# Half of an encoder block's output projection by Strassen's seven products, the sums of weights made by accumulating DMAs

## The chip, the cores and the metric

The kernel runs on one core of a Trainium2 chip. The metric is the device time of one execution in microseconds; the time of the kernel before is the median of three runs, 913.6 us (913.25 to 913.76).

## The reference

One layer of a hybrid encoder block on 256 tokens of width 2048, in float32:

```
xn     = rms_norm(x, norm_pre_w)
z      = xn @ w_in                       # 2048 x 13312: u, g_lru, q, k, v, g_attn, m_lru, m_attn
y_a    = rg_lru(conv(u)) * silu(g_lru)   # both directions, added
y_b    = windowed_gqa(q, k, v) * silu(g_attn)
merged = sigmoid(m_lru) * (y_a @ w_proj_a) + sigmoid(m_attn) * (y_b @ w_proj_b)
x      = x + rms_norm(merged @ w_out, norm_post_w)
```

The change concerns `merged @ w_out` (256 x 2048 by 2048 x 2048) and what surrounds it. The last norm needs the sum of squares of a token's whole row of 2048, so nothing of a token's output can be written before its last column is there.

## The kernel before

Every float32 operand of a matmul is cut in two float32r parts, high and low (`parts_of`, `split`), and each product is three matmuls (`mm3`, L165: high by high, high by low, low by high). ScalarE (ACT) casts the high part, VectorE (DVE) subtracts for the low part.

The program is a list of steps, one for each 1 MB load of weights in `load_plan`, in the order in which TensorE (PE) uses them. A step has two half-steps; PE works on one half (1024 columns of the loaded tile) in each. The loop at the end of `body` writes the program out half-step by half-step: `fetch` issues the load of three steps ahead on SyncE's (SP's) queue, into a ring of three buffers `raw`; then come the callbacks that are due at this half-step (`at`, `soon`); then `split` cuts the half that is four half-steps ahead into `wh` and `wl`, rings of five buffers; then the matmuls. Each engine takes its own instructions strictly in that order.

`add_rows` adds a column chunk of 512 of a projection with tokens as rows: four steps of kind "quad", each of which holds four blocks of 128 rows of the weights; per step 4 blocks x 2 halves of the tokens x 3 = 24 matmuls of 128x512. It takes two PSUM banks for a chunk, from the ring of four single banks `bg` (`bank`, `spare=True`) or as one of two double tiles `mm` (`banks`).

The end of the program, in order: chunks of `w_proj_b` (`add_pb`) alternate with the last gates (`add_ma`). After each `w_proj_b` chunk, `turn` transposes the merged tile on PE in two pieces into a `bg` bank `mt` and cuts it into the tiles `ms` (eight in all: 256 rows of the contraction by 256 tokens, high and low part), which are the operand of the output projection. Then four chunks `o0` to `o3` of `w_out` follow (16 steps, tile name `o`), each evacuated by `o_evac`: ACT squares with a running sum (`junk`, L723), DVE multiplies by the norm's weight (`yw`, L726). In the last chunk the matmuls of the second half of the tokens come after the first half's are complete (`held`), so that the first half's ending runs beside them. The ending of a token half is a square root, a reciprocal and four scaled additions of the input rows `xr` (L738), each with its output DMA. `load_tail` loads `npt` and `xr` from the second half-step of the projection on. Tiles of 4 KB a partition are taken from the pool `u` of 31 units; a unit that is reused waits for its last reader.

Of the kernel before, what the change touches and what calls it, by code (L numbers as in the profile page):

```python
# [14 lines left out]
F32 = mybir.dt.float32  # L15
F32R = mybir.dt.float32r
# [4 lines left out]
P = 128  # L21
# [21 lines left out]
       ("w_proj_a", 1536), ("w_in", MA0), ("w_in", MA0 + 512)]  # L43


PV_NORM = 0
PV_CW = 16
PV_CB = PV_CW + 64
# [7 lines left out]
def load_plan():  # L56

    plan = []

    def quad(m, c):  # L60
        plan.extend(("quad", m, c, i) for i in range(4))

    def pair(m, c, n):
        plan.extend(("blk", m, c + (n + i) * P, 0) for i in range(2))

    quad("w_in", U0)
    for i in range(8):
# [19 lines left out]
    for c in range(4):  # L87
        quad("w_out", c * 512)
    return plan


def body(ctx, tc, x, xT, wall, wlru, pvec, npost, ident_d, mask_d, rope_d, out):
# [8 lines left out]
    def unit(name, dt=F32, shape=(P, 4, S)):  # L101
        return units.tile(list(shape), dt, tag="u", name=name)
# [17 lines left out]
    def parts_of(h, l, src, cast=nc.scalar.copy):  # L120
        cast(h, src)
        nc.vector.tensor_tensor(l, src, h.bitcast(F32), ALU.subtract)
# [8 lines left out]
    def at(hs, fn):  # L131
        assert hs >= now[0], (hs, now[0])
        due.setdefault(hs, []).append(fn)
# [8 lines left out]


    raws, parts = {}, {}

    def fetch(i):
# [3 lines left out]
        nc.sync.dma_start(raws[i], wall[i])  # L150

    def split(q, c=0, w=1024, cast=nc.scalar.copy, only=None):
        i, h = q // 2, q % 2
        if i >= len(plan):
            return
        if c == 0 and only != "l":
            parts[q] = [ring.tile([P, 1024], F32R, tag=f"w{s}", name=f"w{s}{i}_{h}", bufs=5) for s in "hl"]
        wh, wl = parts[q]
        hs, ls, raw = wh[:, c:c + w], wl[:, c:c + w], raws[i][:, h * 1024 + c:h * 1024 + c + w]
        if only != "l":  # L160
            cast(hs, raw)  # L161
        if only != "h":
            nc.vector.tensor_tensor(ls, raw, hs.bitcast(F32), ALU.subtract)  # L163
# [41 lines left out]
    def add_rows(name, act, done, spare=False, last=False):  # L205


        got, held = [], []

        def products(t, g, h, wh, wl):  # L210
            ts = slice(t * P, (t + 1) * P)
            for j in range(2):
                k = 4 * g + 2 * h + j
                sl = slice(j * 512, (j + 1) * 512)
                a = act[k // 2][:, k % 2, :, ts]
                mm3(got[t], a[:, 0], a[:, 1], wh[:, sl], wl[:, sl], k == 0, k == KT - 1)

        def half(g, h, wh, wl):
            if g == 0 and h == 0:
                if spare:  # L220
                    got.extend(bank(f"{name}{t}", (P, 512)) for t in range(2))
                else:
                    ps = banks(name, (P, 2, 512))
                    got.extend(ps[:, t] for t in range(2))
            products(0, g, h, wh, wl)
            if last and g >= 2:
                held.append((1, g, h, wh, wl))
            else:
                products(1, g, h, wh, wl)
            if g == 3 and h == 1:  # L230
                if last:
                    done(0, got[0])
                    for a in held:
                        products(*a)
                    done(1, got[1])
                else:
                    soon(lambda: [done(t, got[t]) for t in range(2)])

        for g in range(4):
            steps.append(("quad", lambda h, wh, wl, g=g: half(g, h, wh, wl)))  # L240


    pv = const.tile([P, PV_N], F32, name="pv")
# [267 lines left out]
            nc.vector.tensor_tensor(dst, dst, sg, ALU.mult)  # L511
        return done

    tm, sm, ms = [], [], []


    def gate_evac(units_list, c):
# [146 lines left out]
    def add_pb(c):  # L664
        def done(t, ps):
            g = sm[c][:, t]
            nc.vector.tensor_tensor(g, ps, g, ALU.mult)
            nc.vector.tensor_tensor(g, tm[c][:, t], g, ALU.add)
            if t == 1:
                for i in range(2):  # L670
                    soon(lambda i=i: turn(i), i + 1)

        def turn(i):

            ps = bank(f"mt{c}{i}")
            for j in range(2):
                sl = slice((2 * i + j) * P, (2 * i + j + 1) * P)
                for t in range(2):
                    nc.tensor.transpose(ps[:, j, t * P:(t + 1) * P], sm[c][:, t, sl], ident)
            m = pair_unit(f"ms{2 * c + i}")  # L680
            ms.append(m)
            parts_of(m[:, :, 0], m[:, :, 1], ps)

        add_rows(f"pb{c}_", yb, done)

# [19 lines left out]

    def load_tail():
        for h in range(2):
            sl = slice(h * 1024, (h + 1) * 1024)
            npt.append(unit(f"np{h}", F32, (P, 1024)))
            nc.sync.dma_start(npt[h], npost[:, sl])  # L710
            for t in range(2):
                xr[t].append(unit(f"xr{t}{h}", F32, (P, 1024)))
                yw[t].append(unit(f"yw{t}{h}", F32, (P, 1024)))
                nc.sync.dma_start(xr[t][h], x[t * P:(t + 1) * P, sl])

    at(2 * len(steps) + 2, load_tail)

    def o_evac(c):
        def done(t, ps):
            cs = slice((c % 2) * 512, (c % 2 + 1) * 512)  # L720
            junk = small.tile([P, 512], F32, tag="p", name=f"junk{c}{t}", bufs=2)
            sums, bb = so[t], bias[t]
            nc.scalar.activation(junk, ps, AF.Square, accum_out=sums[:, c:c + 1])  # L723
            if c == 3:
                nc.scalar.activation(bb, sums[:, 3:4], AF.Sqrt, scale=1.0 / D, bias=bb)
            nc.vector.tensor_tensor(yw[t][c // 2][:, cs], ps, npt[c // 2][:, cs], ALU.mult)  # L726
            if c == 2:
                nc.vector.tensor_tensor(sums[:, 0:1], sums[:, 0:1], sums[:, 1:2], ALU.add)
                nc.vector.tensor_tensor(sums[:, 0:1], sums[:, 0:1], sums[:, 2:3], ALU.add)
                nc.vector.tensor_scalar(bb, sums[:, 0:1], 1.0 / D, EPS, ALU.mult, ALU.add)  # L730
                if t == 1:
                    nc.scalar.activation(warm, eps, AF.Sqrt)
            if c == 3:
                nc.vector.reciprocal(bb, bb)
                for q in range(4):
                    cs = slice((q % 2) * 512, (q % 2 + 1) * 512)
                    y = yw[t][q // 2][:, cs]
                    nc.vector.scalar_tensor_tensor(y, y, bb, xr[t][q // 2][:, cs], ALU.mult, ALU.add)  # L738
                    eng = nc.sync if q % 2 == 0 else nc.scalar
                    eng.dma_start(out[t * P:(t + 1) * P, q * 512:(q + 1) * 512], y)  # L740
        return done

    for c in range(4):
        add_rows(f"o{c}_", ms, o_evac(c), True, c == 3)


    assert [s[0] for s in steps] == [p[0] for p in plan]
    for i, (_, half) in enumerate(steps):
        for h in range(2):
            now[0] = hs = 2 * i + h  # L750
            if h == 0:
                fetch(i + 3)
# [16 lines left out]

def pack_weights(w):  # L770
    loads = []
    for kind, m, c, i in load_plan():
        if kind == "quad":
# [58 lines left out]
```

## Time and profile before

| | |
|---|---|
| median of three runs | 913.6 us |
| the profiled execution, its own time | 914.62 us |
| its span, first to last instruction | 912.8 us |
| PE busy | 903.2 us (99%), 4790 matmuls |
| DVE busy | 650.6 us (71%) |
| ACT busy | 534.7 us (59%) |
| GpSimd (POOL) busy | 1.4 us |
| DMA | 172.20 MB, mean 189 GB/s |
| granted TensorE clock | 0.998 |

Engines work at the same time, so the busy times are not to be added. Matmuls are pipelined: one is shown as 0.39 us long, but the next starts before it ends, so what a matmul costs PE is the distance between two starts. The span leaves out 1.8 us of the profiled execution's time, before the first and after the last instruction.

### The profile page before, as it was taken

To read this page: it belongs to the slowest core of one execution; us is meant where nothing else is said; L and a number is where in the kernel's file an instruction comes from. 1 tells how busy PE (TensorE), PEld (TensorE's weight loads), DVE (VectorE), ACT (ScalarE), POOL (GpSimd) and SP (SyncE) were. 2 spreads that over 40 slices of the span, in tenths; PEclk is the share of its full clock that TensorE was granted. 3 is DMA by queue.
4 is the path that set the end of the run, shared out by engine and by line. 5 is a ranking of instruction groups with operands and counts; after the bars stand their busy time and mean duration, and the time that the engine had idled before them with its cause. 6 is when DMAs were issued, how large, how long until landed. Compare 5 with 4: busy or idle time off the path is not lost.

```text
span 912.8 us, 12138 instructions
## 1 busy us (share of the span) xinstructions
PE 903.2 (99%) x4790; PEld 775.5 (85%) x4790; DVE 650.6 (71%) x900; ACT 534.7 (59%) x744; POOL 1.4 (0%) x23
## 2 busy tenths in 40 slices
PE   8999999999999999999999999999999999999996
PEld 8898888888888888888888888888888888888885
DVE  6976968697879888898687868666555555555554
ACT  7678586859497967855644545644464434344451
POOL 0000000000000000000000000000000000000000
PEclk9999999999999999999999999999999999999999
DMA  9764465445464454456544445454555555558532
GB/s 334 257 236 170 162 223 185 165 181 208 155 238 174 162 207 150 154 215 230 186 163 159 145 179 174 150 179 145 183 191 201 183 204 182 191 192 315 185 139 92
DMA packets 27609, 172.20 MB, mean 189 GB/s; under 512 B 3072, under 2 KB 3840, under 8 KB 8480
## 3 DMA queue, kind: packets, MB, share of 16 engines
q1 hardware_dynamic: 26688, 170.14, 52.5%
q10 hardware_dynamic: 864, 1.29, 0.4%
q8 instruction: 37, 0.61, 0.3%
q14 instruction: 20, 0.16, 0.1%
HBM read 169.32 MB, written 2.10 MB: 188 GB/s over the span
## 4 chain that ended last, share of the span: by engine, by line
PE 98%; DMA 1%; DVE 0%; ACT 0%; DVEq 0%; ACTq 0%; issue 0%
PE ga L190 7%; PE q L190 7%; PE gl L190 6%; PE u L190 5%; PE o L166 4%; PE o L167 4%; PE o L168 4%; PE ga L189 3%; PE q L189 3%; PE gl L189 3%; PE u L189 2%; PE u_ps L358 2%; PE k L190 2%; PE gate L166 1%; PE gate L167 1%; PE gate L168 1%
## 5 line engine op out<-in xcount | busy, mean ns | idle before, releaser
L163 DVE TENSOR_TENSOR wl<-raw,wh 128x1024 fp32r<-128x1024 f32 (+1 forms) x306 | 370.1, 1214 | 206.6 <-ACT wh L161 206.1
L161 ACT CAST wh<-raw 128x1024 fp32r<-128x1024 f32 (+1 forms) x305 | 315.5, 1045 | 202.5 <-PE o L168 33.1
L190 PE MATMUL ga<-xs,wh 128*128 128x512 f32 x256 | 90.1, 396 | 0.0
L190 PE MATMUL q<-xs,wh 128*128 128x512 f32 x256 | 89.7, 396 | 0.0
L190 PE MATMUL gl<-xs,wh 128*128 128x512 f32 x224 | 78.9, 397 | 0.0
L190 PE MATMUL u<-xs,wh 128*128 128x512 f32 x192 | 67.6, 396 | 0.0
L189 PE MATMUL ga<-xs,wl 128*128 128x256 f32 x240 | 67.2, 280 | 0.0
L189 PE MATMUL q<-xs,wl 128*128 128x256 f32 x240 | 67.0, 279 | 0.0
L189 PE MATMUL gl<-xs,wl 128*128 128x256 f32 x210 | 58.9, 280 | 0.0
L190 PEld LDWEIGHTS ga<-xs,wh 128*128 128x128 f32 x256 | 47.5, 188 | 10.0
L190 PEld LDWEIGHTS q<-xs,wh 128*128 128x128 f32 x256 | 47.3, 188 | 9.9
L189 PE MATMUL u<-xs,wl 128*128 128x256 f32 x180 | 50.4, 280 | 0.0
L166 PE MATMUL o<-wh,ms 128*128 128x512 f32 x128 | 50.0, 391 | 0.0
L168 PE MATMUL o<-wh,ms 128*128 128x512 f32 x128 | 49.8, 389 | 0.0
L167 PE MATMUL o<-wl,ms 128*128 128x512 f32 x128 | 49.8, 389 | 0.0
L190 PEld LDWEIGHTS gl<-xs,wh 128*128 128x128 f32 x224 | 41.6, 188 | 8.9
L189 PEld LDWEIGHTS ga<-xs,wl 128*128 128x128 f32 x240 | 45.3, 189 | 0.7
L189 PEld LDWEIGHTS q<-xs,wl 128*128 128x128 f32 x240 | 45.3, 189 | 0.7
L190 PEld LDWEIGHTS u<-xs,wh 128*128 128x128 f32 x192 | 35.6, 188 | 7.5
L189 PEld LDWEIGHTS gl<-xs,wl 128*128 128x128 f32 x210 | 39.7, 189 | 0.6
L606 ACT ACTIVATE p<-p,nm 128x256 f32<-128x256 f32 x32 | 16.0, 502 | 37.9 <-DVE nm L604 37.9
L189 PEld LDWEIGHTS u<-xs,wl 128*128 128x128 f32 x180 | 34.0, 189 | 0.5
(338 smaller groups left out, 1978.1 us busy)
## 6 DMA issues: line engine op xcount, KB each, us to landing
raw<-wall_dram SPq DMA_DIRECT2D x149, 1024.0 KB, 4.8
lraw<-wlru_dram SPq DMA_DIRECT2D x8, 512.0 KB, 5.7
raw<-wall_dram SPq DMA_DIRECT2D x4, 512.0 KB, 7.5
xr<-x_dram SPq DMA_DIRECT2D x4, 512.0 KB, 10.3
raw<-wall_dram SPq DMA_DIRECT2D x4, 256.0 KB, 4.8
xT<-xT_dram SPq DMA_DIRECT2D x4, 256.0 KB, 7.2
np<-npost_dram SPq DMA_DIRECT2D x2, 512.0 KB, 7.9
out_dram<-yw SPq DMA_DIRECT2D x4, 256.0 KB, 2.3
```

The costliest lines, as they stand in the source:

```text
L161: cast(hs, raw)
L163: nc.vector.tensor_tensor(ls, raw, hs.bitcast(F32), ALU.subtract)
L166: nc.tensor.matmul(ps, wh, xh, start=start, stop=False)
L167: nc.tensor.matmul(ps, wh, xl, start=False, stop=False)
L168: nc.tensor.matmul(ps, wl, xh, start=False, stop=stop)
L189: nc.tensor.matmul(ps[:, 1], wl[:, sl], a[:, 0], start=False, stop=False)
L190: nc.tensor.matmul(ps, wh[:, sl], a, start=k == 0, stop=k == KT - 1)
L358: nc.tensor.matmul(ups[b // 2][:, b % 2, 0], w[:, sl], a[:, m], start=k == 0 and n == 0, stop=k == KT - 1 and n == 2)
L606: nc.scalar.activation(p[:, t], p[:, t], AF.Exp, bias=nm[:, t:t + 1], accum_out=dn[:, t:t + 1])
```

## The change

Columns 0 to 1023 of the output projection, which were chunks 0 and 1, are computed by Strassen's scheme (in Winograd's form). Tokens are halved (128 and 128), the contraction is halved (the even and the odd blocks of 128), and the columns are halved (0 to 511 and 512 to 1023). Seven products of a 128 x 1024 operand by a 1024 x 512 sum of weights replace eight. Each product is two steps of kind "part" with 12 matmuls of 128x512 each (`Seven.half`), so the 16 steps of the projection become 8 quads (chunks 2 and 3) and 14 parts. `OUT` writes out their order.

Operand sums (s1 to s4) are built from each transposed tile in `turn` (`sums_of`: one ACT copy, three DVE operations, and a cut into parts). Sums of weights: all signs are put into the operands, so that the weights are only added. The products m1 and m2 use one block as it is (kind "z", through the ring `raw`). The chain `x` starts with the block of m1 and is added to for m5, m6 and m4 in turn; the chain `y` starts with the block of m3 and is added to for m7. A chain has two cells for each of its two steps (`x0a`, `x0b`, `x1a`, `x1b`, and the same for `y`), 512 KB each, units of the pool. It is started by plain DMAs on SP and added to by DMAs on POOL's queue with `accum_op=ALU.add`. The chain `x` up to m5's sum is made during the last two chunks of `w_proj_b`; the adds for m6, m7 and m4 are issued as soon as the split of the sum before has been read.

Each product has one `bg` bank. `Seven.after` combines products: m1 is copied to SBUF; with m6, u = m6 + m1 and v = m5 + u are made, and the four outputs are m2 + m1, m3 with v, m5 with u (u now with m7 added), and m4 with u. m5's bank is held until m7 is there, and chunk 3 takes two `bg` banks from its first step on; chunk 2 takes a double tile `mm`. The loads of `npt` move seven steps later and those of `xr` to the third step from the end.

```
+OUT = ("2.0 m1.0 2.1 m1.1 2.2 m5.0 m5.1 m3.0 2.3 m3.1 m6.0 m6.1 3.0 m2.0 m2.1 m7.0 3.1 m7.1 m4.0 m4.1 3.2 3.3")
...
+    def load(cell, p, add=False):
+        w = wall[row[content(p)]]
+        for h in range(2):
+            if add:
+                nc.gpsimd.dma_start(flat(cell[h]), w[:, h * 1024:(h + 1) * 1024], accum_op=ALU.add)
+            else:
+                nc.sync.dma_start(flat(cell[h]), w[:, h * 1024:(h + 1) * 1024])
...
+    def chain_load(i):
+        a, q = plan[i][3:]
+        if a in ("m6", "m7", "m4"):
+            load(chains[SEVEN[a][1], q], plan[i], True)
+        raws[i] = chains[SEVEN[a][1], q]
...
+    def sums_of(name, src):
+        a = src.rearrange("p a b -> p (a b)")
+        a11, a12, a21 = (a[:, i * P:(i + 1) * P] for i in (0, 2, 1))
+        f = half_unit(f"{name}f", "uu", F32).rearrange("p a (b c) -> p (a b) c", b=2)
+        t = unit(name, F32R, (P, 4, 2, P))
+        ends = src.rearrange("p a (b c) -> p (a b) c", b=2)[:, 0:4:3]
+        nc.scalar.copy(f[:, 3], a21)
+        nc.vector.tensor_tensor(f[:, 0:2], ends, f[:, 3].unsqueeze(1).to_broadcast([P, 2, P]), ALU.subtract)
+        nc.vector.scalar_tensor_tensor(f[:, 2], f[:, 1], -1.0, a11, ALU.mult, ALU.subtract)
+        nc.vector.scalar_tensor_tensor(f[:, 3], f[:, 2], -1.0, a12, ALU.mult, ALU.subtract)
+        parts_of(t[:, :, 0], t[:, :, 1], f)
+        return t
...
+        def half(self, m, q, h, wh, wl):
+            fresh, last = q == 0 and h == 0, q == 1 and h == 1
+            if fresh:
+                self.ps[m] = bank(f"{self.name}{m}", (P, 512))
+            for j in range(2):
+                ah, al = self.rows(SEVEN[m][0], 4 * q + 2 * h + j)
+                sl = slice(j * 512, (j + 1) * 512)
+                mm3(self.ps[m], ah, al, wh[:, sl], wl[:, sl], fresh and j == 0, last and j == 1)
+            if last:
+                soon(lambda: self.after(m))
...
+        def after(self, m):
+            ps, done = self.ps, self.done
+            if m == "m1":
+                self.m1 = half_unit(f"{self.name}c", "lo", F32, 1).rearrange("p a b -> p (a b)")
+                nc.scalar.copy(self.m1, ps.pop("m1"))
+            elif m == "m2":
+                done(0, 0, ps.pop("m2"), self.m1, 1)
+            elif m == "m6":
+                self.u = self.temp("u")
+                nc.vector.tensor_tensor(self.u, ps.pop("m6"), self.m1, ALU.add)
+                v = self.temp("v")
+                nc.vector.tensor_tensor(v, ps["m5"], self.u, ALU.add)
+                done(0, 1, ps.pop("m3"), v, -1)
+            elif m == "m7":
+                nc.vector.tensor_tensor(self.u, ps.pop("m7"), self.u, ALU.add)
+                done(1, 1, ps.pop("m5"), self.u, -1)
+            elif m == "m4":
+                done(1, 0, ps.pop("m4"), self.u, 1)
...
+    for q in range(2):
+        at(2 * len(steps) - 16 + 4 * q, lambda q=q: chain_start(("part", "w_out", 0, "m1", q), "x"))
+        at(2 * len(steps) - 12 + 4 * q, lambda q=q: load(chains["x", q], ("part", "w_out", 0, "m5", q), True))
+        at(2 * len(steps) - 4 + 4 * q, lambda q=q: chain_start(("part", "w_out", 0, "m3", q), "y"))
...
+    def o_sum(t, c, ps, other, sign):
+        f = small.tile([P, 512], F32, tag="p", name=f"of{t}{c}", bufs=2)
+        nc.vector.scalar_tensor_tensor(f, ps, float(sign), other, ALU.mult, ALU.add if sign > 0 else ALU.subtract)
+        o_done(t, c, f)
```

Two places of the engines' order matter for the prediction. The first is DVE between two chunks or products of the projection. Before, at the passage from chunk 0 to chunk 1 (`wl` is the low part of a step's half, `raw` its load, `o0_0` and `o0_1` the chunk's two banks, `yw` the evacuation):

```order
L163 TENSOR_TENSOR wl140_1_7394<-raw140_7317,wh140_1_7393 128x1024
L163 TENSOR_TENSOR wl141_0_7412<-raw141_7375,wh141_0_7411 128x1024
L163 TENSOR_TENSOR wl141_1_7428<-raw141_7375,wh141_1_7427 128x1024
L726 TENSOR_TENSOR yw00_7322<-o0_0_7279,np0_7319 128x512
L726 TENSOR_TENSOR yw10_7325<-o0_1_7280,np0_7319 128x512
L163 TENSOR_TENSOR wl142_0_7452<-raw142_7409,wh142_0_7451 128x1024
```

Now, at the passage from m2 (bank `om2`) to m7, where `oc` is m1's copy, `of00` one output chunk, and `wl151`, `wl152`, `wl153` the steps m7.0, 3.1 and m7.1:

```order
L229 TENSOR_TENSOR wl151_0_7750<-y0a_7263,wh151_0_7749 128x1024
L229 TENSOR_TENSOR wl151_1_7761<-y0b_7264,wh151_1_7760 128x1024
L229 TENSOR_TENSOR wl152_0_7773<-raw152_7745,wh152_0_7772 128x1024
L229 TENSOR_TENSOR wl152_1_7783<-raw152_7745,wh152_1_7782 128x1024
L895 SCALAR_TENSOR_TENSOR of00_7792<-om2_7753,oc_7483 128x512
L877 TENSOR_TENSOR yw00_7587<-of00_7792,np0_7585 128x512
L879 TENSOR_TENSOR so0_169<-so0_169 128x1
L880 TENSOR_TENSOR so0_169<-so0_169 128x1
L881 TENSOR_SCALAR ob0_171<-so0_169 128x1
L229 TENSOR_TENSOR wl153_0_7801<-y1a_7335,wh153_0_7800 128x1024
```

The reading of a finished product stands behind the split of the half that is four half-steps on, as the evacuation did before; a split's source is now a chain's cell (`y0a`, `y0b`) or a `raw` buffer, and four half-steps are shorter where steps are parts.

The second place is POOL's queue. Before, its last rows are clearings of the edges of `upad`, long ahead of the projection, and the program's end:

```order
L368 MEMSET upad_2557 128x2
L367 MEMSET upad_2912 128x2x2 [waits DVE_49,Pool_49]
L368 MEMSET upad_2912 128x2
L827 UNCONDITIONAL_BRANCH
L827 ISA [waits barrier_Pool_Activation_PE_DVE_SP_gather]
```

Now the adds stand there, 16 of 512 KB each; these are the last twelve (m6 into `x`, m7 into `y`, m4 into `x`), with the semaphores for which each waits (DVE: the split that read the cell; DMASW, DMAHW: the add or plain load that filled it):

```order
L185 DMA x0a_7006<-wall_dram 128x1024 [waits DMASW0_49,DVE_49]
L185 DMA x0b_7007<-wall_dram 128x1024 [waits DMASW1_49,DVE_49]
L185 DMA x1a_7084<-wall_dram 128x1024 [waits DMASW2_49,DVE_49]
L185 DMA x1b_7085<-wall_dram 128x1024 [waits DMASW3_49,DVE_49]
L185 DMA y0a_7263<-wall_dram 128x1024 [waits DMAHW0_49,DVE_49]
L185 DMA y0b_7264<-wall_dram 128x1024 [waits DMAHW1_49,DVE_49]
L185 DMA y1a_7335<-wall_dram 128x1024 [waits DMAHW4_49,DVE_49]
L185 DMA y1b_7336<-wall_dram 128x1024 [waits DMAHW5_49,DVE_49]
L185 DMA x0a_7006<-wall_dram 128x1024 [waits DMASW4_49,DVE_49]
L185 DMA x0b_7007<-wall_dram 128x1024 [waits DMASW5_49,DVE_49]
L185 DMA x1a_7084<-wall_dram 128x1024 [waits DMASW6_49,DVE_49]
L185 DMA x1b_7085<-wall_dram 128x1024 [waits DMASW7_49,DVE_49]
```

POOL now carries every add in one line: an add that waits holds up those behind it.

More of the change, by code (lines that the diff above doesn't have):

```diff
@@ new lines, in body, with __init__, add, rows @@
+    class Seven:
+        def __init__(self, name, act, sums, done):
+            self.name, self.act, self.sums, self.done = name, act, sums, done
+            self.ps = {}
+        def add(self, m, q):
+            steps.append(("part", lambda h, wh, wl: self.half(m, q, h, wh, wl)))
+        def rows(self, a, i):
+            if a[0] == "a":
+                t, b = int(a[1]) - 1, int(a[2]) - 1
+                src = self.act[i][:, b, :, t * P:(t + 1) * P]
+            else:
+                src = self.sums[i][:, SUMS.index(a)]
+            return src[:, 0], src[:, 1]
+        def half(self, m, q, h, wh, wl):
[8 more added lines that the diff above has]
+                soon(lambda: self.after(m))
+        def temp(self, name):
+            return small.tile([P, 512], F32, tag="uu", name=f"{self.name}{name}", bufs=2)
+        def after(self, m):
[16 more added lines that the diff above has]
+                done(1, 0, ps.pop("m4"), self.u, 1)
@@ L512, in silu_evac @@
         return done
-    tm, sm, ms = [], [], []
+    tm, sm, ms, msum = [], [], [], []
     def gate_evac(units_list, c):
@@ L716, in body @@
[L716 to L741, printed above, removed]
@@ new lines, in o_sum @@
+    def o_sum(t, c, ps, other, sign):
+        f = small.tile([P, 512], F32, tag="p", name=f"of{t}{c}", bufs=2)
+        nc.vector.scalar_tensor_tensor(f, ps, float(sign), other, ALU.mult, ALU.add if sign > 0 else ALU.subtract)
+        o_done(t, c, f)
+    seven = Seven("o", ms, msum, o_sum)
+    orows = {}
+    for o in OUT.split():
+        a, i = o.split(".")
+        if a in SEVEN:
+            seven.add(a, int(i))
+        elif i == "0":
+            c = int(a)
+            n = len(steps)
+            add_rows(f"o{c}_", ms, lambda t, ps, c=c: o_done(t, c, ps), c == 3, c == 3)
+            orows[a] = steps[n:]
+            steps[n:] = [orows[a].pop(0)]
+        else:
+            steps.append(orows[a].pop(0))
```

97 lines of the change are left out of this document (83 added, 14 removed).

## The prediction

> **What bounds the kernel now.** I read the page first: its busy times, and the chain of work that ended last.
>
> ```profile
> span 912.8 us, 12138 instructions
> PE 903.2 (99%) x4790; PEld 775.5 (85%) x4790; DVE 650.6 (71%) x900; ACT 534.7 (59%) x744; POOL 1.4 (0%) x23
> PE 98%; DMA 1%; DVE 0%; ACT 0%; DVEq 0%; ACTq 0%; issue 0%
> ```
>
> PE is busy for 99% of the span and makes 98% of the chain: only fewer matmuls, or new gaps between them, can move the time. The second view is the instructions on the projection's tile `o` (first and last start), then the timeline in the middle of it and at two passages, all engines.
>
> ```profile
> L166 PE MATMUL o<-wh,ms x128: 389/389/478, 817.1 to 904.7; 128*128 128x512 f32 x128
> 850.75 0.39 PE L168 MATMUL o<-wh,ms 128*128 128x512 f32 x1
> 850.97 0.39 PE L166 MATMUL o<-wh,ms 128*128 128x512 f32 x1
> 851.17 1.05 ACT L161 CAST wh<-raw 128x1024 fp32r<-128x1024 f32 x1 [1.67 <-PE o L168]
> 851.20 0.39 PE L167 MATMUL o<-wl,ms 128*128 128x512 f32 x1
> ...
> 852.26 1.22 DVE L163 TENSOR_TENSOR wl<-raw,wh 128x1024 fp32r<-128x1024 f32 x1 [1.49 <-ACT wh L161]
> 853.24 0.39 PE L167 MATMUL o<-wl,ms 128*128 128x512 f32 x1
> ```
>
> The projection's matmuls start at 817.1. From the matmul at 851.20 to that at 853.24 there are nine steps of 0.227 us: that, not 0.39, is a matmul's price. A quad step is 24 of them, 5.44 us; a half-step 2.72 us. The timeline also shows the machinery of the splits: ACT waits for PE to finish a half-step (the matmul at 850.75, which ends at 851.14), because only then a `wh` buffer is free, casts until 852.22, and DVE subtracts until 853.48. A split is thus done 2.51 us after its half-step began at 850.97, and before the half-step is over: today it costs PE nothing.
>
> For the transfers, the windows (their last two columns are the busy share of the DMA engines and GB/s), then the median time from issue to landing:
>
> ```profile
> 772.00:817.00 45.00, 45.00 (x203) 37.04 (x202) 23.79 (x23) 18.99 (x20) 0.00 (x0) 1.00 0.54 187
> 817.00:839.00 22.00, 22.00 (x102) 17.94 (x101) 12.89 (x14) 9.47 (x11) 0.00 (x0) 1.00 0.92 335
> 839.00:906.00 67.00, 66.53 (x294) 54.77 (x292) 33.43 (x39) 27.61 (x38) 0.00 (x0) 1.00 0.40 141
> raw<-wall_dram SPq DMA_DIRECT2D x149, 1024.0 KB, 4.8
> ```
>
> At a share of 0.92 they moved 335 GB/s, so a full share is 364 GB/s and a load of 1 MB (1.049 million bytes) takes 2.9 us of all engines; the other 1.9 of the 4.8 us is fixed. Transfers have room: half the share in the merge, 0.40 in the projection's rest.
>
> **The change: what PE saves.** Fourteen part steps of 12 matmuls and eight quads of 24 are 360 matmuls in place of 384: 24 x 0.227 = **5.4 us less**. The distance stays, since shapes and operands are alike. Nothing else on PE goes.
>
> **What it adds under cover.** Prices of the added work, from groups of instructions of like shape:
>
> ```profile
> L163 DVE TENSOR_TENSOR wl<-raw,wh 128x1024 fp32r<-128x1024 f32 x302 | 367.4, 1221 | 205.9 <-ACT wh L161 205.4
> L161 ACT CAST wh<-raw 128x1024 fp32r<-128x1024 f32 x302 | 313.7, 1049 | 201.4 <-PE o L168 33.1 <-PE q L190 14.1 <-PE ma__6065 L168 12.6
> L122 DVE TENSOR_TENSOR ms<-mt,ms 128x512 fp32r<-128x512 f32 x8 | 5.5, 692 | 4.6 <-ACT ms L121 4.1
> L121 ACT CAST ms<-mt 128x512 fp32r<-128x512 f32 x8 | 4.7, 587 | 16.0 <-PE mt L679 16.0
> L636 DVE TENSOR_TENSOR sg<-o,sg 128x256 f32<-128x256 f32 x16 | 6.7, 417 | 0.0
> L333 DVE TENSOR_TENSOR diag<-rbc,ident 128x128 f32<-128x128 f32 x2 | 0.6, 288 | 0.5 <-ACT diag L334 0.5
> L582 DVE SCALAR_TENSOR_TENSOR vl<-v_ps,rtok,vh 128x512 fp32r<-128x512 f32 x2 | 1.5, 751 | 0.8 <-ACT vh L581 0.8
> L334 ACT ACTIVATE diag<-diag 128x128 f32<-128x128 f32 x2 | 0.6, 310 | 3.8 <-DVE diag L333 3.8
> ```
>
> - Operand sums, for each of eight tiles: DVE 0.42 + 0.29 + 0.29 + 0.69 = 1.7 us, ACT 0.31 + 0.59 = 0.9 us. Six tiles fall in the merge, where DVE is busy 23.8 of 45 us: hidden. The last two delay DVE by 3.4 us at the projection's start; four half-steps of splits stand ahead there, so PE sees nothing. Without that cover it would be up to 3.4 us.
> - Twelve more splits: DVE 14.7, ACT 12.6 us, beside PE. In a part step a half-step is 6 x 0.227 = 1.36 us, and DVE needs 1.22 of it, so DVE just keeps up but has no slack there; this returns below.
> - Combinations: four at 0.75 (L582) and three at 0.69 on DVE, one copy on ACT: 5.1 and 0.6 us, beside PE except at the three places below.
> - In the merge: 3 MB of plain loads on SP and 2 MB of adds. 45 us at a share of 0.54 leave 45 x 0.46 = 20.7 us of the DMA engines; 3 x 2.9 + 2 x 2.9 = 14.5 us are asked, 20.3 if an add costs double. Hidden, but the `raw` loads behind the chains' on SP land later; if a split comes late for it, PE loses at most the one or two loads ahead, 3 to 6 us. I take 0.
> - The tail: chunk 3 is still last, with the same evacuation and outputs; `xr` now lands near the end but before its use. 0.
>
> **What it puts on the path: three hand-overs of a bank.** The ring `bg` has four banks. From chunk 3's first step two of them hold `o3`, and m5's result holds a third until m7 is added. So m2, m7 and m4 share the fourth, one after the other, and `OUT` lets them follow each other directly: m2.1 m7.0, and m7.1 m4.0 (with 3.1 in the middle of m7, which doesn't free anything). PE must wait until DVE has read m2 (`of00`) or m7 (`ou`), with all of PE's later work behind it; and DVE reads only after the split ahead of it in its order. By the rows above that split is done 2.51 us after the start of the product's last half-step, which lasts 1.36 us: 1.15 us after PE's last start there would be followed by the next. Then the reading, 0.75 for m2 or 0.69 for m7, then the way back to PE:
>
> ```profile
> 819.37 0.69 DVE L668 TENSOR_TENSOR mg<-mg,mg 128x512 f32<-128x512 f32 x1
> ...
> 820.12 0.31 PEld L679 LDWEIGHTS mt<-ident,mg 128*128 128x128 f32 x3 [0.36 <-DVE mg L668]
> ```
>
> DVE's end at 820.06 and PE's start at 820.12 make it 0.06. So 1.15 + 0.75 + 0.06 = **1.96 us** for m2 to m7, **1.90** for m7 to m4. The third: chunk 3's second bank is m6's. After m6.1 PE has six matmuls on the first bank (1.36 us) while DVE needs 1.15 + 0.69 + 0.06 = 1.90: 0.54 if DVE has no backlog; chunk 2's evacuation (2 x 0.69) just before leaves up to 1.4 more. I take **1.0**. Sum 4.9. The bounds: where DVE is free when a product ends, only the end of the last matmul (0.39 - 0.23 = 0.16), the reading and the way back remain, 0.97 and 0.91, and 0 for the third: 1.9 in all. With a backlog of one split (1.22) at each of the first two and the full 1.9 at the third, 8.2.
>
> **What may come on the path: the adds.** No accumulating DMA is in the trace. The last six MB (m6, m7, m4) can be issued once m5's split has read the cells. m1.1 begins 1.1 (two sets of transposes) + 5.44 + 2.72 + 5.44 = 14.7 us after 817.1; its second half 1.4 later; with 2.5 for the split and about 1.5 of DVE's delay: 837. The last, m4.1, must have landed when its second half is cast, in the second half of m7.1: 62.6 us of steps + 1.4 + 1.1 + 3 of waits after 817.1, 885. Of these 48 us 1.9 is fixed: 46. SP's queue has five 1 MB loads and 2 MB of `xr` in that time, 7 x 2.9 = 20. So 26 us are left for 6 MB. At the plain load's 2.9 us a MB (lower bound: the same bytes come from HBM and go to SBUF) they take 17.4, 9 to spare. At three such passes (two reads and a write, one after the other: upper bound) 52, 26 late. I take up to 4.3 us a MB, so no wait: what is added to the plain load is a read of SBUF, and the row it is nearest to is the plain load's.
>
> On this the Trainium skill speaks against the change: "Collectives: The Full Stack", in the section on the bandwidth ceiling and the fold count, says that a transfer which adds is slower because it reads two sources through one ring, and gives about half the rate of a copy. By that rule 6 MB would take an estimated 35 us, 9 more than the 26 left; no run here shows it yet. It is the second rival below.
>
> **The sum.** Against the profiled execution's own 914.6 us: 914.6 - 5.4 + 4.9 = 914.1. The median of the runs is 1.0 below that execution (913.6), so **913.1 us**. The bounds of the hand-overs make it 910.1 to 916.4; most of that range's weight lies within 911.8 and 915.4. A difference of 0.2% (1.8 us) is about what a measurement of this kernel can tell from no change.
>
> **Rivals.**
> 1. *Cheap hand-overs*: DVE stands free at each product's end. 913.6 - 5.4 + 1.9 = **910.1**. Against it: ACT starts each cast only when PE ends a half-step (the wait of 1.67 us in the timeline), so the split can't be early. 0.12.
> 2. *Adds at half the rate* (**slower**): the point from which it decides is 26 / 6 = 4.3 us a MB. At 5.8 they are 34.8 - 26 = 9 late, or 3 if `xr` lets them pass. The wait shows before m4: DVE's order puts the reading of m7 behind the split of m4.1, so m4's first matmul waits for m4.1's landing. 913.1 + 3 to 9 = 916 to 922, **920** for the most part. For it: two reads per byte written; against: room at a share of 0.40. 0.27.
> 3. *Adds much slower than that*, by the engines or by the time POOL takes to issue twelve: at three passes 913.1 + 20 to 26, **936**. For it: POOL's issue is not in the trace at all; against: twelve issues have 48 us. 0.15.
>
> That the change doesn't save the matmuls is no rival: 360 stand in its order.
>
> **How the numbers follow.** The forecast has 0.46: 0.36 of it within 0.2%, 0.05 each side beyond. Faster: 0.12 + 0.05 = **0.17**. Same: **0.36**. Slower: 0.27 + 0.15 + 0.05 = **0.47**. Cases of both signs hold most of the chance, so the forecast's own range is 910.1 to 916.4; the range for 8 in 10 runs from 910.5, which leaves out a part of rival 1, to 928, which takes in rival 2 and leaves out rival 3 but its lowest part.
>
> **What would show it.** Right: 24 fewer matmuls at 0.227; PE idle by 1.5 to 2.5 us before the first `om7` and before the first `om4`, released by DVE, and by 0.5 to 2 before `o3_1`; no wait of ACT's casts for a DMA; adds landing before 885. Wrong: casts of `x0a` to `x1b` that wait for the adds, and a wait before `om4` far above 2 us (rival 2 or 3); waits at the hand-overs of 1 us or less (rival 1); new waits of PE in the merge (the SP queue) or at the projection's start (the sums).

## The result, and the profile after

The changed kernel takes 914.95 us (median of 20 runs, 914.13 to 915.55), the kernel before beside it 914.14 (median of 20): a ratio of 1.0006, 95% interval 0.9999 to 1.0013. That is 0.8 us more, an interval that takes in no change at all, and inside the 0.2% that count as none. The forecast was 913.1 from a base of 913.6, so 0.5 less than the kernel before. The profiled execution took 914.77 us, the one before 914.62.

The head of the page of the changed kernel, with the chain that ended last:

```profile
span 913.0 us, 12250 instructions
PE 898.9 (98%) x4766; PEld 770.8 (84%) x4766; DVE 681.5 (75%) x951; ACT 552.7 (61%) x773; POOL 15.5 (2%) x39
PE 96%; DVE 1%; DMA 1%; ACT 1%; issue 0%; DVEq 0%; ACTq 0%
```

The 24 matmuls are gone (4766 in place of 4790), and PE's share of the chain fell from 98% to 96%, so other engines now stand on the path. How much they cost is best read from PE's own two ends of the projection: the first and the last matmul, in the timeline of the kernel before,

```profile
817.12 0.39 PE L166 MATMUL o<-wh,ms 128*128 128x512 f32 x1
905.14 0.39 PE L168 MATMUL o<-wh,ms 128*128 128x512 f32 x1
```

and in that of the changed one:

```profile
816.34 0.39 PE L232 MATMUL o__7347<-wh,ms 128*128 128x512 f32 x1
904.41 0.39 PE L234 MATMUL o<-wh,ms 128*128 128x512 f32 x1
```

Before, they lie 88.03 us apart, now 88.07. PE gained nothing at all: 5.44 us of matmuls were taken out and 5.4 us of gaps put in. (That both stand 0.75 us earlier goes back to the start of these two executions: the hundredth matmul of the program is at 16.95 and 16.12, and between 15.6 and 18.7 in the profiles of this study. Spans of single executions are therefore compared by their parts below.) The gaps are in the view of PE's waits, from the start of the merge on; before, the same view was empty:

```profile
PE om L232 <- DVE of L895: 1.7, 1, 1.7
PE om L232 <- DVE ou L375: 1.7, 1, 1.7
PE o L232 <- DVE ou L369: 1.2, 1, 1.2
```

These are the three hand-overs of a bank, and nothing else. The first in the timeline, m2 to m7:

```profile
872.01 2.54 DVE L229 TENSOR_TENSOR wl<-raw,wh 128x1024 fp32r<-128x1024 f32 x2
872.24 1.06 ACT L227 CAST wh<-raw 128x1024 fp32r<-128x1024 f32 x1 [0.26 <-PE om L234]
873.17 0.39 PE L234 MATMUL om<-wh,ms 128*128 128x512 f32 x1
874.47 0.68 DVE L895 SCALAR_TENSOR_TENSOR of<-om,oc 128x512 f32<-128x512 f32 x1
875.30 0.47 PE L232 MATMUL om<-wh,mx 128*128 128x512 f32 x1 [1.74 <-DVE of L895]
875.60 0.40 PE L233 MATMUL om<-wl,mx 128*128 128x512 f32 x1
```

m2's last matmul starts at 873.17. DVE is then in the split for two steps on, until 874.55; only then does it read m2, until 875.15, and m7's first matmul starts at 875.30. The wait counts from the modelled end of a matmul (0.39 long). By distances of starts the cost is more: 2.13 + 0.30 for two steps that take 0.227 each, so 1.98 us. The second hand-over is alike, 1.98; the third, by the same count, 1.46 (1.57 + 0.34 - 0.45). Together 5.42.

What is left of the difference is the program's end. From the last matmul's start to the span's end it was 7.67 us, and now it is 8.54. The tail's arithmetic has not changed: DVE's last operation ends 4.68 us after that matmul in both. The rest is SP's list of waits for semaphores and the program's end behind it. In the view of SP's waits in the last microseconds, before,

```profile
SPq L827 <- DMA out_dram<-yw: 2.2, 4, 0.7
SPq L827 <- PEq L827: 0.6, 2, 0.4
```

and after:

```profile
SPq L997 <- DMA out_dram<-yw: 2.3, 4, 0.9
SPq L997 <- PEq L997: 1.1, 2, 1.0
```

The outputs' landing is waited for as before; what follows, where SP waits for the other engines to end, is 0.5 longer, and SP's list has ten instructions that wait for semaphores in place of six. By the times in the trace, SP is through its list 0.31 us later: the last output lands 0.07 later, and four waits of 0.06 stand behind the one for it, where none stood before. The other 0.56 come after that, on POOL. Its first instruction DRAIN in the program's end starts 0.34 later after SP is through than in the kernel before, and takes 0.24 in place of 0.08. So the sum closes: - 5.44 + 5.42 + 0.87 = + 0.85, where the medians give + 0.81.

The windows of the changed kernel (busy time of PE, PEld, DVE, ACT and POOL, granted clock, DMA share, GB/s) answer to those of before:

```profile
772.00:817.00 45.00, 45.00 (x202) 36.99 (x202) 27.06 (x31) 20.72 (x25) 3.63 (x4) 1.00 0.94 305
817.00:839.00 22.00, 22.00 (x101) 18.00 (x100) 18.45 (x24) 12.68 (x17) 2.60 (x3) 1.00 0.72 261
839.00:906.00 67.00, 61.13 (x266) 49.33 (x265) 49.53 (x57) 38.12 (x50) 7.83 (x9) 1.00 0.75 202
```

In the merge the DMA share rose from 0.54 to 0.94 and PE still has no gap. In the rest of the projection it went from 0.40 to 0.75, and that is a mean: from 835 to 880 it is full.

### The profile page after: what moved, and what is told of

Read it like the earlier page. It is cut to its first block, busy times and chain, and to the rows that moved or that the text cites. A ratio compares the mean times of both kernels' runs of the same rounds, so it can differ in the third digit from the quotient of the medians.

```text
span 913.0 us, 12250 instructions
## 1 busy us (share of the span) xinstructions
PE 898.9 (98%) x4766; PEld 770.8 (84%) x4766; DVE 681.5 (75%) x951; ACT 552.7 (61%) x773; POOL 15.5 (2%) x39
## 4 chain that ended last, share of the span: by engine, by line
PE 96%; DVE 1%; DMA 1%; ACT 1%; issue 0%; DVEq 0%; ACTq 0%
PE ga L256 7%; PE q L256 7%; PE gl L256 6%; PE u L256 5%; PE ga L255 3%; PE q L255 3%; PE gl L255 3%; PE u L255 2%; PE u_ps L496 2%; PE k L256 2%; PE o L232 1%; PE o L234 1%; PE o L233 1%; PE om L232 1%; PE om L234 1%; PE om L233 1%
## 5 line engine op out<-in xcount | busy, mean ns | idle before, releaser
L229 DVE TENSOR_TENSOR wl<-raw,wh 128x1024 fp32r<-128x1024 f32 (+1 forms) x298 | 358.7, 1214 | 164.4 <-ACT wh L227 163.3
L227 ACT CAST wh<-raw 128x1024 fp32r<-128x1024 f32 (+1 forms) x297 | 305.7, 1044 | 156.8 <-PE q L256 14.1
L648 ACT ACTIVATE sig<-sg 128x512 f32<-128x512 f32 x16 | 10.1, 632 | 34.6 <-DVE sg L511 34.6
L568 DVE SCALAR_TENSOR_TENSOR uu<-upad,pv,uu 128x256 f32<-128x256 f32 x48 | 23.3, 485 | 2.3
L256 PE MATMUL k<-xs,wh 128*128 128x512 f32 x64 | 22.5, 398 | 0.0
```

Of the source, the lines that this page charges most:

```text
L256: nc.tensor.matmul(ps, wh[:, sl], a, start=k == 0, stop=k == KT - 1)
L568: nc.vector.scalar_tensor_tensor(u, up[:, j, tap:tap + S], cw[:, tap:tap + 1], u, ALU.mult, ALU.add)
L648: nc.scalar.activation(sg, dst, AF.Sigmoid)
```

## The experiments

**Chunk 3's banks from the other pool.** The three gaps should go if each product has a bank of its own.

```
-                if spare:
+                if last:
+                    got.extend(banks(f"{name}{t}", (P, 512)) for t in range(2))
+                elif spare:
```

> The two accumulators of chunk 3 are taken from the other pool of banks, so that all four banks of `bg` are left to the products and no product has to wait for another's reading. Theory (the saving of PE is given back at three hand-overs of a bank, 1.7 + 1.7 + 1.2 = 4.6 us by the trace of the changed kernel): the three waits are gone, the time is 4.0 to 4.7 us below the changed kernel, some 910.4, and the last adds still land before their cast, with 1 to 2 us to spare in place of 4. Rival (the saving is lost on PE for another reason, or the adds set the pace from behind the hand-overs): the waits move to the casts of the last sums or to other places and the time falls by less than 2 us.

Measured: 909.85 us (before 914.07; ratio 0.9957, 0.9944 to 0.9969), 5.1 below the changed kernel by the medians. The hand-overs are the cause: the three waits are gone and PE's stretch, from its first to its last matmul of the projection, is 83.60 us, 4.47 shorter. One new wait is left, which costs 0.99 by distances:

```profile
PE o L233 <- DVE wl L229: 0.7, 1, 0.7
```

In the timeline of ACT, the casts of m4's last two sums:

```profile
880.15 1.05 ACT L227 CAST wh<-x1a 128x1024 fp32r<-128x1024 f32 x1 [1.41 <-PE o L234]
882.54 1.05 ACT L227 CAST wh<-x1b 128x1024 fp32r<-128x1024 f32 x1 [1.34 <-DVE wl L229]
```

The profile puts the pause before 882.54 down to DVE, but the last add, `x1b`, landed at 882.44 by its record in the trace, and PE had ended the half-step that frees the cast's buffer near 881.4. With the gaps gone the adds seem to be 1.1 us late, where 1 to 2 us to spare were expected. The last two runs below test that.

**The banks as they were, another order.**

```
-3.0 m2.0 m2.1 m7.0 3.1 m7.1 m4.0 m4.1 3.2 3.3
+3.0 m2.0 m2.1 3.1 m7.0 m7.1 3.2 m4.0 m4.1 3.3
```

> The banks stay as they are; only the order is changed: step 3.1 stands between m2 and m7, and step 3.2 between m7 and m4, so that PE has 5.4 us of other matmuls while DVE reads the finished product. Theory (hand-overs): the waits before om7 and om4 go, that before o3_1 (1.2 us) stays: 3.4 us below the changed kernel, some 911.5; m7's and m4's adds have the more time by one step. Rival (the bank isn't what PE waits for, but DVE's backlog or the splits): DVE's backlog is the same, waits of 1.5 us or more appear at other matmuls, and the time falls by less than 1.5 us.

Measured: 910.95 us (before 914.07; ratio 0.997, 0.9959 to 0.9982), 4.0 below the changed kernel. The wait that stays is the third:

```profile
PE o L232 <- DVE ou L369: 1.2, 1, 1.2
```

4.0 is twice 1.98: the price of a hand-over is the distance of the starts, not the 1.7 of the wait, which is why the expectation was low.

**The product read ahead of the split.** In the last half-step of m2.1 and m7.1 (`late`):

```
-                split(hs + 4)
+                split(hs + 4, only="h" if late else None)
...
+            if late:
+                at(hs + 1, lambda q=hs + 4: split(q, only="l"))
```

> In the last half-step of m2 and of m7 DVE's part of the split ahead is put behind the reading of the finished product; ACT's part stays. Theory (the prediction's working of a hand-over: 1.15 us of it are the split that stands ahead of the reading): each of the two waits falls from 1.7 to about 0.9 us (0.16 for the end of the last matmul, the reading of 0.6 to 0.7, the way back), 1.4 to 1.9 us below the changed kernel, some 913.2. Rival (the wait is DVE's general backlog, or the reading itself and the way to it): the waits stay within 0.4 us of 1.7, no change; or the late split stalls PE one half-step later and gives it back.

Measured: 913.33 us (before 914.07; ratio 0.999, 0.9982 to 0.9999), 1.6 below the changed kernel:

```profile
PE om L232 <- DVE of L895: 0.9, 1, 0.9
PE om L232 <- DVE ou L375: 0.9, 1, 0.9
```

The split ahead of the reading is 0.86 us of each hand-over; 1.12 by distances (1.98 before) is what a bank passed directly from one product to the next still costs where no split stands ahead of the reading.

**Both remedies of the first two runs.** The edits are those above, together:

```
+                if last:
+                    got.extend(banks(f"{name}{t}", (P, 512)) for t in range(2))
...
+3.0 m2.0 m2.1 3.1 m7.0 m7.1 3.2 m4.0 m4.1 3.3
```

> Both remedies at once: chunk 3's accumulators from the other pool of banks, and the order with 3.1 before m7 and 3.2 before m4. Theory (after the banks are free nothing of the hand-overs is left but a wait of 0.7 us of PE for a low part, which comes from DVE's backlog of short steps; the order spreads those): 0 to 0.7 us below the run with the banks alone, 909.2 to 909.9, with one step more for m4's adds, 3 us or more to spare. Rival (the order's only use was to hide the hand-overs): equal within 0.3 us, the same wait of 0.7 us.

Measured: 910.24 us (before 914.02; ratio 0.9959, 0.9946 to 0.9973), no better than with the banks alone: PE's stretch is 83.53, 0.07 shorter, and the end behind it 0.22 longer (8.76 against 8.54). The rival is nearer: the wait of 0.7 is gone, but small ones elsewhere cost as much, 0.36 and 0.57 by distances. Ahead of the first of them a `raw` load is late, as the view of ACT's waits has it:

```profile
ACT wh L227 <- DMA raw<-wall_dram: 2.2, 1, 2.2
```

**The adds as plain loads on POOL.**

```
-nc.gpsimd.dma_start(flat(cell[h]), w[:, h * 1024:(h + 1) * 1024], accum_op=ALU.add)
+nc.gpsimd.dma_start(flat(cell[h]), w[:, h * 1024:(h + 1) * 1024])
```

> The sixteen adds stay on POOL's queue, with the same waits and bytes, but as plain loads: the sums of weights are left out, a cell simply holds the block that came last. Theory (in the changed kernel the adds land 4 us or more before their use and cost no time of their own): within 0.4 us of the changed kernel, the three waits of PE at 1.7, 1.7 and 1.2 us as before; the loads land at the plain rate, 512 KB in 1.3 us of all DMA engines in place of 2.5, and the last one some 8 us earlier. Rival (the adds' traffic holds up other loads or the end of the program): 1 us faster or more.

Measured: 915.04 us (before 914.02; ratio 1.0012, 1.0003 to 1.0021), the same three waits, so in the changed kernel the adds cost no time on the path. The last load landed 15.9 us earlier than the last add, counted from the projection's start, where 8 were expected. What an add costs the DMA engines stands in the rows of POOL's queue in the two pages (packets, MB, share of 16 engines), of the changed kernel and of this one:

```profile
q0 software_dynamic: 2304, 8.39, 4.8%
```
```profile
q0 software_dynamic: 2304, 8.39, 2.7%
```

The same bytes take 1.8 times as much of the engines. By landings one behind the other, m6's four adds came 2.47 us apart (841.89 to 849.31) and the same four as plain loads 1.27: 4.9 us a MB against 2.5, a factor of 1.9. Nothing else moved in these stretches, and the DMA engines were full (shares of 1.05 and 1.02). The 4.3 that the prediction granted an add was too low, and its 2.9 for a plain load too high.

**The same plain loads on SP.**

```
-nc.gpsimd.dma_start(flat(cell[h]), w[:, h * 1024:(h + 1) * 1024], accum_op=ALU.add)
+nc.sync.dma_start(flat(cell[h]), w[:, h * 1024:(h + 1) * 1024])
```

> As in the run with plain loads on POOL, but issued on SP's queue: POOL issues no DMA at all; the sums of weights are left out here too. Theory (the 0.9 us by which the program's end takes longer come from POOL's DMA queue being used with its eight semaphores): the end shrinks to that of the kernel before, 0.6 to 0.9 us faster than with the loads on POOL. Since a single DMA on POOL in the kernel before moved nothing, the rival is that the end goes by other things (the order of the last outputs): the same time within 0.3 us. A wait of SP for a cell would hold its `raw` loads up; those are issued three steps ahead, so that a wait of PE for them would be new and would show as ACT's casts waiting for a DMA.

Measured: 914.38 us (before 914.02; ratio 1.0004, 0.9995 to 1.0013), 0.66 below the run with them on POOL. From the last matmul's start to the end it is 8.0 us, on POOL 8.55, in the kernel before 7.67. SP's last waits:

```profile
SPq L997 <- DMA out_dram<-yw: 2.5, 2, 2.0
SPq L997 <- PEq L997: 0.6, 2, 0.4
```

The second row is back to the 0.6 of the kernel before: between these two kernels the half microsecond goes with the queue that issues the loads. The 0.3 that are left are SP's: as in the changed kernel, four waits stand behind the one for the last output.

**One DMA on POOL, and eight, in the kernel before.**

```
-    at(6, lambda: nc.sync.dma_start(ident, ident_d))
+    at(6, lambda: nc.gpsimd.dma_start(ident, ident_d))
```

> The kernel before, with one change: the small load of `ident` goes out on POOL's queue, the only DMA there. It tests the end of the program, which took about 0.9 us longer in the changed kernel, by a longer list of semaphores and a later end of POOL. Theory (using POOL's DMA queue at all lengthens the program's end, whatever is issued there): 0.4 to 0.9 us slower than the kernel before, with POOL's last instructions later after the last output. Rival (the end's length goes by the last outputs' transfers or by the number of POOL's DMAs, eight of whose semaphores the changed kernel uses): within 0.3 us of the kernel before.

```
-    at(6, lambda: nc.sync.dma_start(ident, ident_d))
+    def load_ident():
+        for i in range(8):
+            nc.gpsimd.dma_start(ident[16 * i:16 * i + 16], ident_d[16 * i:16 * i + 16])
+    at(6, load_ident)
```

> The kernel before, with the load of `ident` cut into eight pieces of 16 rows, all on POOL's queue. With the loads on SP the changed kernel ended 0.6 us sooner after its last matmul than with them on POOL, while one DMA on POOL added only 0.1 us to the kernel before. Theory (the cost is one of POOL's DMA semaphores each, of which the changed kernel uses eight): the end after the last matmul's start grows from 7.7 to about 8.2 to 8.5 us, 0.4 to 0.8 us slower than the kernel before. Rival (the cost comes from the adds' size or number, or from their being near the end): within 0.2 us of the kernel before, the end at 7.7 to 7.8 us.

Measured: 914.25 us with one (ratio 1.0002, 0.9993 to 1.0011) and 914.42 with eight (1.0005, 0.9996 to 1.0014); the end after the last matmul is 7.8 us in both profiles, against 7.67. The median with eight, 0.35 above its kernel before, lies between the theory's 0.4 and the rival's 0.2 and within the noise; the end is what decides. Neither theory held: it is not the use of the queue as such nor its eight semaphores. Nor do number and size of the DMAs decide alone: the next run has twenty of 512 KB on POOL's queue, 10.5 MB, the last landing 21 us ahead of the last matmul, and its end is 8.0 us long, with the short wait,

```profile
SPq L999 <- PEq L999: 0.6, 2, 0.5
```

while this wait is 1.1 in all eight profiles with sixteen, whether the last of them landed 39 us ahead of the last matmul (the plain loads) or 17 (the banks alone). What decides is open.

**m4's adds twice.**

```
         if a in ("m6", "m7", "m4"):
             load(chains[SEVEN[a][1], q], plan[i], True)
+        if a == "m4":
+            load(chains[SEVEN[a][1], q], plan[i], True)
```

> The four adds of m4 are issued twice (the sums of m4 are then not those of the reference), 2 MB more of adds at the end of POOL's queue. It tests the deadline that the prediction set for the adds. Theory (the last add has 4.2 us to spare in the changed kernel, and an add of 512 KB takes 2.5 us of the DMA engines where it has them alone, up to 5 where it shares them with the loads): the last lands 10 to 14 us later, 6 to 10 us too late, ACT's cast of `x1a` and `x1b` waits for it and PE with it before om4: 5 to 10 us slower than the changed kernel. Rival (there is far more room than that, since transfers overlap): no change within 1 us.

Measured: 927.81 us (before 914.02; ratio 1.0154, 1.014 to 1.0168), 12.9 above the changed kernel, beyond the expectation. The place is the one that was named: PE before om4 waits 13.5 in place of 1.7 for DVE's reading of m7, which stands behind the split of m4.1 and so behind ACT's cast:

```profile
PE om L234 <- DVE ou L377: 13.5, 1, 13.5
```
```profile
ACT wh L229 <- DMA x1a<-wall_dram: 10.7, 1, 10.7
```

The DMA engines were full in this time (windows with PE's busy time, granted clock, DMA share, GB/s):

```profile
880.00:885.00 5.00, 5.00 (x24) 1.00 1.05 270
885.00:890.00 5.00, 2.54 (x12) 1.00 1.07 275
890.00:895.00 5.00, 0.00 (x0) 0.58 0.95 225
```

The last add landed 15.8 us later than in the changed kernel, counted from the projection's start, where 10 to 14 were expected. The 2 MB more account for 9.9 at 4.9 us a MB. The rest, argued and not measured apart, fits the order: in the timeline of POOL the second add into a cell waits for the first one's landing, and holds up those behind it:

```profile
862.84 0.86 POOL L185 DMA_DIRECT2D x0b<-wall_dram  x1 [1.61 <-DVE wl L231]
869.80 0.86 POOL L185 DMA_DIRECT2D x0a<-wall_dram  x1 [6.09 <-DMA x0a<-wall_dram]
```

A first add took 9 to 13 us from issue to landing, and POOL stood 3 to 8 us before each second one. So all of `xr` landed ahead of the last two adds (892.95 against 895.40 and 897.88), its 2 MB some 5 us at the plain load's 2.5. The deadline comes out as the expectation had it: 15.8 less the 4.2 us to spare is 11.6, and the distance before om4 grew by 11.75. Another 1.6 us are PE's matmuls behind the pause, six of them at distances of 0.43 in place of 0.23.

**m4 one step earlier.** On the kernel with chunk 3's banks in the other pool:

```
-m7.0 3.1 m7.1 m4.0 m4.1 3.2 3.3
+m7.0 m7.1 m4.0 m4.1 3.1 3.2 3.3
```

> The kernel with chunk 3's accumulators in the other pool, and step 3.1 put behind m4.1, so that m7 and m4 follow each other and PE wants m4's sums one step of 5.4 us earlier. It tests the adds' deadline with nothing else changed: in the kernel with the banks alone the last add (`x1b`) landed at 882.44 and its cast began at 882.54, 1.1 us after a buffer was free for it. Theory (the adds stand exactly at their deadline there, at some 4.9 us a MB): the cast waits for the add by some 6 us less what the later `raw` loads leave free, PE loses 2.5 to 6 us more than in the kernel with the banks alone, 912.5 to 916, and the wait before om4 is put down to the add. Rival (the adds' landing and the cast only happen to fall together, and transfers spread by themselves): within 1 us of 909.9.

Measured: 917.27 us (before 914.06; ratio 1.0031, 1.0019 to 1.0043; six runs from 915.1 to 919.3), 7.4 above the kernel with the banks alone: the theory's sign and place, and 1.3 us beyond its range. In the views of ACT's waits and of windows (PE's busy time, granted clock, DMA share, GB/s) of the execution profiled, the longest of the six:

```profile
ACT wh L227 <- DMA x1b<-wall_dram: 3.1, 1, 3.1
```
```profile
890.00:895.00 5.00, 4.83 (x11) 0.50 0.00 0
```

The cast waits for the add as expected. PE's stretch grew by 6.3 us to 89.87: 1.8 in m4, 3.2 at the passage to chunk 3, and 2.2 which neither theory had, since after these gaps eleven matmuls follow at distances of 0.43 in place of 0.23, at a granted clock of 0.50; less the 0.99 of the kernel with the banks alone, which is in these gaps now. The profiled execution is 9.2 us longer than that of the kernel with the banks alone: another 2.6 of it lie ahead of the projection's first matmul, where nothing was changed, so this one trace doesn't close the 7.4 of the medians.

**`xr` behind the last cast.** On the kernel with chunk 3's banks in the other pool:

```
-nc.sync.dma_start(xr[t][h], x[t * P:(t + 1) * P, h * 1024:(h + 1) * 1024])
+nc.scalar.dma_start(xr[t][h], x[t * P:(t + 1) * P, h * 1024:(h + 1) * 1024])
...
-    at(2 * (len(steps) + len(OUT.split())) - 6, load_rows)
+    at(2 * (len(steps) + len(OUT.split())) - 4, load_rows)
```

> The kernel with chunk 3's accumulators in the other pool; the 2 MB of `xr` go out on ACT's queue behind its last cast, at about 891, where they were issued on SP from 870 on beside the last four adds. Theory (in the kernel with the banks alone the last adds share the DMA engines with `xr` and land 1 us late): `x1b` lands 2 to 5 us earlier, its cast no longer waits, and the gap of PE of 0.9 + 0.1 us at chunk 3's step 3.2 is gone: 0.6 to 1.0 us below that kernel, some 909.0; `xr` lands by 898 and may cost up to 1 us at the tail, where it is first read at 896.9. Rival (the gap is DVE's backlog of short steps, not the add): the gap stays, 909.9 or, with a late `xr`, more.

Measured: 909.43 us (before 914.06; ratio 0.9952, 0.9939 to 0.9965). PE has no wait left from the merge to the end; its first and last matmul of the projection, and the cast of `x1b`:

```profile
816.44 0.39 PE L232 MATMUL o__7347<-wh,ms 128*128 128x512 f32 x1
899.04 0.39 PE L234 MATMUL o<-wh,ms 128*128 128x512 f32 x1
881.74 1.05 ACT L227 CAST wh<-x1b 128x1024 fp32r<-128x1024 f32 x1 [0.26 <-PE om L234]
```

The stretch is 82.60 us, 5.43 less than before the change: the whole price of 24 matmuls. The add landed 2.5 us earlier, counted from the projection's start, and its cast waits for PE alone. The `raw` loads of the last steps had landed before these casts in both kernels, so the adds are what `xr` had held up. (ACT's queue issued `xr` from 887.25 on, not at 891; the last of it landed at 895.96.) The 0.99 us of the first run were the adds at their deadline. The median's step of 0.4 between these two kernels is too small for their intervals; PE's stretch is what shows it. This kernel beats both: 4.6 us under the kernel before, which is 5.4 less the 0.9 of the program's end.

## Why the forecast came out, step by step

- **24 matmuls at 0.227**: right. 5.43 us were seen where nothing stood against them (the last run).
- **Three hand-overs, 1.96 + 1.90 + 1.0 = 4.9**: right in kind and place, with 1.98, 1.98 and 1.46 measured. That the first came out within 0.02 is partly luck: of its terms the wait for the split measured 1.15 as taken, the reading 0.60 for 0.75, the way back 0.15 for 0.06, and 0.08 fell on the second matmul, for which there was no term. The third was the term mis-sized: 1.46 lies halfway between the 1.0 taken and the 1.9 of its bound, since DVE came to the reading of m6 with more of a backlog than was granted. The composition was right too: putting the reading ahead of the split took 0.86 of the 1.15 ascribed to it.
- **Hidden sums, splits and merge transfers**: right. PE has no wait in the merge or at the projection's start, at a DMA share of 0.94 (0.86 to 0.99 by the prediction's 14.5 to 20.3 us).
- **Adds at no more than 4.3 us a MB, so in time**: the conclusion held, the step did not, and that is luck. An add takes 4.9 us a MB; by the prediction's own sum 6 MB would then need 29.6 of 26 us and be 3.6 late. The room was mis-sized the other way: the adds began at 835.3, not 837, a plain load took 2.5 us a MB, not 2.9, and `xr`, counted as ahead of the last add, landed behind it (882.0 to 885.9 against 880.98). So the last cast, at 885.13, began 4.2 us after its add. On the rate, "Collectives: The Full Stack" of the Trainium skill, in the section on the bandwidth ceiling and the fold count, states half of a copy's for the reduce-scatter of a ring collective, and says that its model holds for rings of three ranks or more; the prediction took it for any transfer that adds. The factor of 1.9 measured here, for loads on one core, comes to the same size. With the banks alone the buffer for that cast was free 3.5 us sooner, as two of the three hand-overs lie ahead of it, and the add landed 1.7 us later, both counted from the projection's start: 1.1 late. Rival 2 had the rate right, and stood hidden behind the hand-overs.
- **The tail at 0**: right for its arithmetic, wrong for the program's end, 0.87 us, a term that the prediction didn't have. 0.31 are SP's, mostly four waits that now stand behind the one for the last output; 0.56 are POOL's end, which was short with the loads on SP and with m4's adds twice, and whose cause stays open. With it and the 0.5 of the hand-overs, the forecast's gain of 0.5 became a loss of 0.8.
- **Cheap hand-overs (rival 1)**: refuted as it stood; even with DVE free a direct hand-over cost 1.12, not 0.97. **Adds slowed by POOL's issue (rival 3)**: an issue takes 0.86 to 1.0 us of POOL and was never late, and the engines took 4.9 us a MB, not the 8.7 of three passes.

## What to carry to other kernels

Where a change saves matmuls but makes products share a bank, price each direct hand-over (end of the split ahead, reading, way back: 2 us here, against 0.23 a matmul) before counting the saving: two banks more or a step of other work in between gave back 4 to 4.5 of 5.4 us. A margin on the path is measured against the slower kernel: once waits are taken away, the next deadline (here the adds') comes nearer by those that lay ahead of it, so check its slack first. An accumulating DMA is to be budgeted at twice a plain load by this case's 1.9, and loads that aren't needed yet are best kept out of its window.

## What the runs showed of the hardware

- An accumulating DMA from HBM into SBUF took 4.9 us a MB where the plain load took 2.5, at a full share of the DMA engines in both (1.05 and 1.02).
- In two runs PE came back from pauses at half clock (0.50 granted): eleven distances of 0.427 us after the gaps of the kernel with m4 earlier, and six after the 13.5 us of the one with m4's adds twice, while in the changed kernel, after gaps of 2 us, the distances are back at about 0.23 from the second one on. "TensorE: Matmul & The Clock Gate" of the Trainium skill, in Part 1, gives 426.7 ns for this shape at the gated clock; the trace agrees.
- With sixteen DMAs of 512 KB on POOL's queue POOL's part of the program's end was some 0.55 us longer, in all eight profiles; with twenty it was not, and with one, or eight small ones, the end grew by 0.1.
